# Making the skewed copies of the bias table: one transfer out of SBUF, or eight from DRAM to DRAM

## The chip, the cores and the metric

The kernel runs on 1 core of one Trainium2 chip. The metric is the device time of one execution in microseconds (us); less is better. TensorE (PE) multiplies, VectorE (DVE), ScalarE (ACT) and GpSimd (POOL) do the elementwise work, and SyncE (SP) issues the DMA transfers of this kernel, which 16 DMA engines carry out.

## The reference

Two transformer blocks run one after the other over 512 tokens of width 1024, all in float32. The first block has two layers (band attention, short convolution, gated mixing, feed-forward). The second has four kinds of attention, two of which add a bias that depends on the distance between query and key and on the head, 8 heads in all:

```python
def _t5_bias(table, dist):
    return jnp.moveaxis(table[_t5_bucket(dist)], -1, -3).astype(jnp.float32)
...
s = jnp.einsum('bhqmd,bhkmd->bhmqk', qb, k) * scale
s = s + _t5_bias(table, dist)[:, None]
s = jnp.where(dist >= 0, s, NEG)
```

The bias of a head is one function of the distance. Written as a row of 640 numbers (float32, 2560 bytes), the bias of a block of 128 queries is that row, shifted by one place from query to query.

## The kernel before

**Weights.** Every weight matrix is cut into units of 128 x 1024 float32 (512 KB). `Stream` loads unit after unit in the order of use into 3 `raw` buffers (L255, on SP's queue), and splits each into a rounded part `wh` on ACT (L267) and a remainder `wl` on DVE (L268). A product of a 128-column block with the activations is 24 matmuls of 128x512 (`mm_kb`, L514 to L516: 8 slices of the inner dimension by three products); `mblock` does that for one unit. `next` splits two units ahead of the one in use, and a `raw` buffer is loaded anew as soon as L268 has read it.

**The stage around the change.** After the first layer's band attention (whose last products run at about 271 us) come `bias_tables` and then the z stage of that layer: 8 column blocks, in each of which `mblock` makes a product, DVE scales it into `z` (L635) and ACT and DVE split the convolution's output `y` into two parts (L506, L507). The sigmoid of the `z` blocks runs on ACT (L378). The second layer has the same z stage, without `bias_tables`.

**The bias table.** `bias_tables` (L846) makes the 8 rows of 640 numbers by a small matmul with a one-hot matrix (L860), and ACT copies them to the tile `row` (L861): 8 partitions with 2560 bytes each. One DMA (L863) then writes 128 copies of each row to the DRAM tile `bias_d` [8, 128, 640], reading each partition of `row` 128 times: 2.6 MB. Much later, in the second block, `load_bias` (L865) reads 4 heads at a time from `bias_d`, with a row step of 639 instead of 640, which shifts each copy by one place.

**What sets the order.** The program writes instructions in the order of the source; a scheduler in the framework then simulates the program and orders each engine's instructions by when they are ready there, with the source order as priority. Each engine, and SP with its DMA issues too, then works through its list in order. DRAM tiles are tracked like others: a DMA that reads one waits on a semaphore until the DMA that wrote it has landed.

Of the kernel before, what the change touches and what calls it, by code (L numbers as in the profile page):

```python
# [9 lines left out]
F32 = mybir.dt.float32  # L10
# [4 lines left out]
P = 128  # L15
# [264 lines left out]
class Kern:  # L280
# [250 lines left out]
    def layer(self, l, tail, pend):  # L531
        nc = self.nc
        h = Pair(self, "h", NB)
# [100 lines left out]
        for m in range(NB):  # L634
            nc.vector.tensor_mul(z[m], self.mblock(h), self.R)  # L635
            self.split(yp.hi[m], yp.lo[m], y[m])
        op_ = Pair(self, "op", NB)
        for m in range(NB):
            self.act(z[m], z[m], AF.Sigmoid)
# [206 lines left out]
    def bias_tables(self):  # L846
        nc = self.nc
        oh = self.blk("oh", [33, 768], F32)
        nc.sync.dma_start(oh, self.a["onehot"])
        tab = self.small("tab", [33, 8], bufs=1)  # L850
        nc.sync.dma_start(tab, self.a["tab"])
        ohr = self.blk("ohr", [33, 768], F32R)
        nc.vector.tensor_copy(ohr, oh)
        tabr = [self.small(n, [33, 8], F32R, bufs=1) for n in ("tabh", "tabl")]
        self.split(*tabr, tab)
        row = self.blk("row", [8, 640], F32)
        for c0, c1, c2 in ((0, 512, 512), (512, 768, 640)):
            ps = self.ps("tb")
            for i, t in enumerate(tabr):
                nc.tensor.matmul(ps[0:8, :c1 - c0], t, ohr[:, c0:c1], start=i == 0, stop=i == 1)  # L860
            nc.scalar.copy(row[:, c0:c2], ps[0:8, :c2 - c0])  # L861
        self.bias_d = self.dramp.tile([8, P, 640], F32, name="bias_d")
        nc.sync.dma_start(self.bias_d, row[:, None, :].to_broadcast([8, P, 640]))  # L863

    def load_bias(self, h0):  # L865
        F = FM(self, "F", 4, F32)
# [856 lines left out]
```

## Time and profile before

| | us |
|---|---|
| median of 3 runs | 2506.98 (2504.95 to 2508.45) |
| the profiled execution's own time | 2510.06 |
| its span, from first to last instruction | 2508.3 |
| PE busy | 2416.4 (96% of the span) |
| DVE, ACT, POOL busy | 1354.6, 991.1, 424.2 |

The times of rows are counted from the start of the span. A chain of waits is followed back from the last instruction of a stretch, at each step to what released it. "Landing" is the time from a DMA's issue until its data is there. In a table by stretches, PEclk is the clock granted to TensorE as a share of full speed and DMA the mean busy share of the 16 DMA engines.

### The profile page before, as it was taken

What the parts mean: (1) busy time and instruction counts of PE and PEld (TensorE: products, weight loads), DVE (VectorE), ACT (ScalarE), POOL (GpSimd) and SP (SyncE); (2) the same over time, 40 slices, a digit from 0 to 9 for tenths busy, and PEclk for the clock granted to TensorE, in tenths of its full rate; (3) what the DMA queues carried; (4) which work ended last, traced back from release to release, by engine and by line L of the source; (5) the groups of instructions that cost most, each with busy time, mean ns of one, the idle gap of its engine ahead of it and who ended that gap; (6) DMA issues with size and microseconds to landing.
All of it is one profiled execution on the core that took longest, in us unless ns stands there. A gap on an engine that the chain in (4) does not pass through costs nothing.

```text
span 2508.3 us, 32433 instructions
## 1 busy us (share of the span) xinstructions
PE 2416.4 (96%) x12648; PEld 2078.5 (83%) x12648; DVE 1354.6 (54%) x2349; ACT 991.1 (40%) x1785; POOL 424.2 (17%) x454
## 2 busy tenths in 40 slices
PE   8999779999999999999999999999898899999999
PEld 7888658898888897888888988888797888988888
DVE  7777343356643258776433666422667686645431
ACT  4555232343223234555323422222276575333320
POOL 3423000121110015231011111100031442000000
PEclk9999989999999999999999999999899999999999
DMA  4222442245523231123323554322321214233250
GB/s 143 93 68 72 87 125 84 85 152 210 185 92 126 93 130 59 64 68 100 118 76 101 174 188 168 101 93 93 111 88 40 79 35 135 85 101 101 93 173 29
DMA packets 84857, 264.33 MB, mean 105 GB/s; under 512 B 9023, under 2 KB 17855, under 8 KB 84704
## 3 DMA queue, kind: packets, MB, share of 16 engines
q1 hardware_dynamic: 84704, 262.27, 31.9%
q8 instruction: 99, 1.62, 0.3%
q14 instruction: 54, 0.44, 0.1%
HBM read 247.03 MB, written 15.20 MB: 105 GB/s over the span
## 4 chain that ended last, share of the span: by engine, by line
PE 90%; DVE 5%; another core or an unknown queue 2%; ACT 2%; POOL 1%; issue 1%; DMA 0%; SPq 0%; DVEq 0%; ACTq 0%; POOLq 0%
PE ps L514 24%; PE ps L516 24%; PE ps L515 24%; PE hd L515 2%; PE hd L516 2%; PE hd L514 2%; PE o L821 1%; PE pt L796 1%; PE tm L998 1%; PE tm L999 1%; PE tm L1000 1%; PE s L772 1%; PE s L771 1%; PE s L1117 1%
## 5 line engine op out<-in xcount | busy, mean ns | idle before, releaser
L268 DVE TENSOR_TENSOR wl<-raw,wh 128x1024 fp32r<-128x1024 f32 x382 | 471.2, 1250 | 385.1 <-ACT wh L267 323.3
L267 ACT CAST wh<-raw 128x1024 fp32r<-128x1024 f32 x382 | 389.9, 1049 | 225.3 <-DMA raw<-in_w_dram 144.3
L514 PE MATMUL ps<-hh,wh 128*128 128x512 f32 x752 | 297.3, 396 | 34.2 <-ACT wh L267 34.2
L516 PE MATMUL ps<-hh,wl 128*128 128x512 f32 x752 | 298.0, 396 | 5.0 <-DVE wl L268 5.0
L515 PE MATMUL ps<-hl,wh 128*128 128x512 f32 x752 | 296.8, 395 | 0.0
L515 PE MATMUL ps<-hfl,wh 128*128 128x512 f32 x640 | 249.4, 390 | 0.0
L514 PE MATMUL ps<-hfh,wh 128*128 128x512 f32 x640 | 249.2, 390 | 0.0
L516 PE MATMUL ps<-hfh,wl 128*128 128x512 f32 x640 | 249.0, 389 | 0.0
L514 PEld LDWEIGHTS ps<-hh,wh 128*128 128x128 f32 x752 | 142.8, 190 | 62.2 <-ACT wh L267 35.1
L516 PEld LDWEIGHTS ps<-hh,wl 128*128 128x128 f32 x752 | 142.6, 190 | 34.5 <-DVE wl L268 7.3
L515 PEld LDWEIGHTS ps<-hl,wh 128*128 128x128 f32 x752 | 142.7, 190 | 27.9
L516 PE MATMUL ps<-hidh,wl 128*128 128x512 f32 (+1 forms) x396 | 145.1, 366 | 0.0
L514 PE MATMUL ps<-hidh,wh 128*128 128x512 f32 (+1 forms) x396 | 144.9, 366 | 0.0
L515 PE MATMUL ps<-hidl,wh 128*128 128x512 f32 (+1 forms) x396 | 144.7, 365 | 0.0
L516 PEld LDWEIGHTS ps<-hfh,wl 128*128 128x128 f32 x640 | 120.2, 188 | 25.0
L378 ACT ACTIVATE pp<-pp,at_nm 128x256 f32<-128x256 f32 (+1 forms) x208 | 114.4, 553 | 66.4 <-DVE at_nm L778 54.3
L515 PEld LDWEIGHTS ps<-hfl,wh 128*128 128x128 f32 x640 | 120.2, 188 | 24.6
L514 PEld LDWEIGHTS ps<-hfh,wh 128*128 128x128 f32 x640 | 120.0, 188 | 24.7
L701 POOL TENSOR_TENSOR gs<-gs,R 128x512 f32<-128x512 f32 x44 | 70.0, 1590 | 379.3 <-ACT gs L378 368.3
L515 PE MATMUL ps<-h3l,wh 128*128 128x512 f32 x320 | 124.5, 389 | 0.0
L516 PE MATMUL ps<-h3h,wl 128*128 128x512 f32 x320 | 124.5, 389 | 0.0
L514 PE MATMUL ps<-h3h,wh 128*128 128x512 f32 x320 | 124.3, 389 | 0.0
(439 smaller groups left out, 5251.9 us busy)
## 6 DMA issues: line engine op xcount, KB each, us to landing
raw<-in_w_dram SPq DMA_DIRECT2D x382, 512.0 KB, 3.7
adaraw<-in_ada_dram SPq DMA_DIRECT2D x48, 512.0 KB, 5.7
xd<-xh SPq DMA_DIRECT2D x24, 256.0 KB, 2.1
xh<-xd SPq DMA_DIRECT2D x24, 256.0 KB, 3.1
xh<-in_x_dram SPq DMA_DIRECT2D x16, 256.0 KB, 4.7
bias_d<-row SPq DMA_DIRECT2D x1, 2560.0 KB
xd<-fg SPq DMA_DIRECT2D x8, 256.0 KB, 3.2
F<-bias_d SPq DMA_DIRECT2D x8, 256.0 KB, 4.3
```

Of the source, the lines that this page charges most:

```text
L267: nc.scalar.copy(hi, raw)
L268: nc.vector.tensor_sub(lo, raw, hi.bitcast(F32))
L378: i = nc.scalar.activation(out, in_, func, **kw)
L514: nc.tensor.matmul(ps[:, t], w[0][:, sl], h.hi[kb][:, t], start=first, stop=False)
L515: nc.tensor.matmul(ps[:, t], w[0][:, sl], h.lo[kb][:, t], start=False, stop=False)
L516: nc.tensor.matmul(ps[:, t], w[1][:, sl], h.hi[kb][:, t], start=False, stop=last)
L701: nc.gpsimd.tensor_mul(g, g, self.R)
L771: nc.tensor.matmul(ps[:, :n], q, KH[g][:, LO[i]:HI[i]], start=True, stop=False)
L772: nc.tensor.matmul(ps[:, :n], q, KL[g][:, LO[i]:HI[i]], start=False, stop=True)
L796: nc.tensor.transpose(bank[:, c0:c0 + P], pslice(h, i)[:, c:c + P], self.ident)
L821: nc.tensor.matmul(ps[:, c0:c1], V[j][:, g * P:(g + 1) * P], t[b][:, a, c0:c1], start=(a == 0 and j == 0), stop=(a == 1 and j == 2))
L998: nc.tensor.matmul(o, h.hi[kb][:, tsl], w[0][:, sl], start=kb == 0 and i == 0, stop=False)
```

## The change

`bias_tables` now writes `row` once to a DRAM tile `row_d` [8, 640] (20 KB). The 128 copies of head h are made by `bias_copy(h)`, a DMA that reads row h of `row_d` 128 times and writes 128 rows of `bias_d` (320 KB). It is called once in each of the 8 column blocks of the first layer's z stage, behind the split of `y`.

```diff
         for m in range(NB):
             nc.vector.tensor_mul(z[m], self.mblock(h), self.R)
             self.split(yp.hi[m], yp.lo[m], y[m])
+            if l == 0:
+                self.bias_copy(m)
...
             nc.scalar.copy(row[:, c0:c2], ps[0:8, :c2 - c0])
+        self.row_d = self.dramp.tile([8, 640], F32, name="row_d")
+        nc.sync.dma_start(self.row_d, row)
         self.bias_d = self.dramp.tile([8, P, 640], F32, name="bias_d")
-        nc.sync.dma_start(self.bias_d, row[:, None, :].to_broadcast([8, P, 640]))
+
+    def bias_copy(self, h):
+        self.nc.sync.dma_start(self.bias_d[h], self.row_d[h:h + 1].to_broadcast([P, 640]))
```

## Rows read from the trace of the kernel before

**Rows 1.** The page: span, and busy time by engine.

```profile
span 2508.3 us, 32433 instructions
PE 2416.4 (96%) x12648; PEld 2078.5 (83%) x12648; DVE 1354.6 (54%) x2349; ACT 991.1 (40%) x1785; POOL 424.2 (17%) x454
```

**Rows 2.** Chain of waits, 250 to 420 us: start, length, what.

```profile
286.30 44.11 another core or an unknown queue
330.43 1.05 ACT wh L267
```

**Rows 3.** Waits, 255 to 360 us: who waited for whom, total, times, longest.

```profile
ACT wh L267 <- DMA raw<-in_w_dram: 47.8, 3, 44.1
...
PE ps L514 <- ACT wh L267: 31.3, 1, 31.3
```

**Rows 4.** PE in order of time: start, length, line, operation, idle before.

```profile
299.80 0.39 PE L516 MATMUL ps<-hh,wl 128*128 128x512 f32 x1
331.53 0.80 PE L514 MATMUL ps<-hh,wh 128*128 128x512 f32 x1 [31.34 <-ACT wh L267]
...
338.19 0.39 PE L514 MATMUL ps<-hh,wh 128*128 128x512 f32 x1
```

**Rows 5.** Stretches: PE, PEld, DVE, ACT, POOL busy; PEclk, DMA, GB/s last.

```profile
300.00:310.00 10.00, 0.19 (x1) 0.00 (x0) 0.00 (x0) 0.00 (x0) 0.00 (x0) 0.68 0.62 102
310.00:320.00 10.00, 0.00 (x0) 0.00 (x0) 0.00 (x0) 0.00 (x0) 0.00 (x0) 0.50 0.46 50
...
340.00:350.00 10.00, 10.00 (x45) 8.26 (x44) 4.96 (x8) 5.98 (x9) 0.00 (x0) 1.00 0.31 103
350.00:360.00 10.00, 10.00 (x46) 8.28 (x45) 8.57 (x11) 5.85 (x9) 0.00 (x0) 1.00 0.78 240
```

**Rows 6.** SP's DMA issues in order of time: start, length of the issue.

```profile
265.91 0.35 SPq L255 DMA_DIRECT2D raw<-in_w_dram  x1
274.36 0.83 SPq L863 DMA_DIRECT2D bias_d<-row  x1
275.46 19.33 SPq L255 DMA_DIRECT2D raw<-in_w_dram  x1
```

**Rows 7.** The tile raw, 275 to 277 us: landing of the load issued there.

```profile
DMA to landing us min/median/max: 54.9/54.9/54.9
```

**Rows 8.** DVE in order of time, first layer's z stage, then the second layer's.

```profile
278.47 0.69 DVE L635 TENSOR_TENSOR z<-ps,R 128x512 f32<-128x512 f32 x1 [3.04 <-PE ps L516]
280.28 2.35 DVE L268 TENSOR_TENSOR wl<-raw,wh 128x1024 fp32r<-128x1024 f32 x2
289.35 0.69 DVE L635 TENSOR_TENSOR z<-ps,R 128x512 f32<-128x512 f32 x1 [4.75 <-PE ps L516]
...
351.34 0.69 DVE L635 TENSOR_TENSOR z<-ps,R 128x512 f32<-128x512 f32 x1
...
1178.41 0.69 DVE L635 TENSOR_TENSOR z<-ps,R 128x512 f32<-128x512 f32 x1 [4.13 <-PE ps L516]
...
1216.49 0.69 DVE L635 TENSOR_TENSOR z<-ps,R 128x512 f32<-128x512 f32 x1
```

**Rows 9.** DMA issues of the page: engine, times, KB each, median us to landing.

```profile
raw<-in_w_dram SPq DMA_DIRECT2D x382, 512.0 KB, 3.7
...
xd<-xh SPq DMA_DIRECT2D x24, 256.0 KB, 2.1
...
bias_d<-row SPq DMA_DIRECT2D x1, 2560.0 KB
...
F<-bias_d SPq DMA_DIRECT2D x8, 256.0 KB, 4.3
...
out_dram<-xm SPq DMA_DIRECT2D x2, 128.0 KB, 1.7
```

**Rows 10.** The tile tab: its load from DRAM.

```profile
L851 SPq DMA_DIRECT2D tab<-in_tab_dram x1: 367/367/367, 7.5 to 7.5; - x1
```

**Rows 11.** ACT in order of time.

```profile
331.38 0.63 ACT L378 ACTIVATE z<-z 128x512 f32<-128x512 f32 x1
```

## The prediction

> **What bounds the kernel now.** I read the page first. PE is busy for 2416.4 of 2508.3 us [rows 1], so only some 92 us of the span can be won by taking waits away, and a change in a transfer is worth what it takes from those 92 us. The list of waits around the bias table shows that a third of them lies here: PE waited once for 31.3 us for the cast of a weight unit (`wh`), and that cast on ACT waited 44.1 us for its `raw` load [rows 3]. The chain of waits says the same: 44.11 us up to 330.43 us that no engine explains, then the cast [rows 2]. SP's list gives the cause. The bias transfer is issued at 274.36, the next weight load at 275.46; that load's issue alone takes 19.33 us [rows 6] and its data is there 54.9 us after issue [rows 7], where the median of the 382 weight loads is 3.7 us [rows 9]. In the stretch in which no engine works (310 to 320 us) the DMA engines are busy for 0.46 of their time and move 50 GB/s [rows 5]: about 7.4 of 16 engines, which fits a transfer of 8 partitions laid on 8 engines, each reading one partition over and over. At 50 GB/s its 2560 KB (2.62 MB) take 52 us, from about 275 to 328. A weight load has its share on those engines too, and stands behind it there.
>
> **What the stall costs.** PE's last matmul before it starts at 299.80, and matmuls follow each other every 0.2267 us at full speed: one block of 24 takes 5.44 us, as the second layer's z stage shows: (1216.49 - 1178.41) / 7 [rows 8]. The next would have started at 300.03. It starts at 331.53, and the first 15 run slowly: the granted clock was 0.50 in the idle stretch and is 1.00 from 340 us on (the levels of 1.2 and 2.4 GHz) [rows 5]. The sixteenth starts at 338.19 [rows 4]; without the stall it would at 300.03 + 15 x 0.2267 = 303.43. The loss is 34.8 us. A second way gives the same: from the first `z` to the eighth the first layer takes 351.34 - 278.47 = 72.87 us, the second, with the same stream of weight loads and no bias transfer, 38.08; the difference is 34.79 [rows 8]. Behind 340 us PE is the bound again, so what is won here arrives at the end.
>
> **The change, part by part.**
>
> *Removed*: the transfer L863, and with it the 34.8 us, if the eight new transfers don't bring part of them back.
>
> *Added: `row_d`*, 20 KB from 8 partitions. It is issued where L863 was, at 274.36, since ACT's copies into `row` are where they were. Nearest rows are stores to DRAM of 128 KB (1.7 us to landing) and 256 KB (2.1 us) [rows 9]; I take 2.
>
> *Added: a wait on SP*. The first copy may only be issued when `row_d` has landed, at about 276.4. SP works in order, so the weight loads listed behind that copy wait up to 2 us as well. PE doesn't see it: after L863 it worked for 25.8 us (274.4 to 300.2) on units loaded before. Seven more DMAs at 0.35 to 0.83 us of issue each [rows 6] are some 3 to 6 us of an SP that has little else to do.
>
> *Moved: the place of the copies*. The source has one in each column block, but a copy waits for nothing except `row_d`, and the scheduler issues what is ready: the load of `tab`, written in `bias_tables`, is issued at 7.5 us [rows 10]. So I expect not a spacing of 5.44 us but most of the eight close together from 276.4 on. The sum must hold in that case too.
>
> *Added: eight copies of 320 KB* (327,680 bytes) from DRAM to DRAM. No row of this trace has such a transfer. From below: the engines moved 240 GB/s at a share of 0.78 [rows 5], so 308 GB/s if all were busy, and a copy holds them for 1.1 us. From above: the share and rate of L863, 50 GB/s at 0.46, scaled to 16 busy engines are 109 GB/s, 3.0 us a copy; and if a copy is spread no better than L863, 50 GB/s, 6.6 us a copy, the same 52 us in all. Which of the two ceilings holds hangs on the spread. A transfer's outermost dimension was 8 in L863 and gave 7.4 busy engines; it is 128 in a copy, as in the weight loads and in the load of `F`, whose 256 KB land after 4.3 us [rows 9], latency included. I take 1.5 us a copy, nearest to the rows of loads and stores with 128 rows, 12 us in all, and keep 1.1 and 6.6 as ends.
>
> The Trainium skill has a rule for the spread: "DMA: Bandwidth & Descriptors", section "Why a DMA increments its semaphore by 16 and not by 1", says that a transfer uses the largest number of engines up to 16 that divides the slowest dimension of both sides, so 8 for L863 and 16 for a copy. The share of 0.46 agrees with its 8; that a step of zero on the source side counts as a dimension of 128 no run here shows yet. By the rule the 6.6 us fall away.
>
> *How much the copies may take before PE notices.* The load issued at 275.46 must land at 298.9 (300.03 less the 1.10 us from the cast's start to PE's, 330.43 to 331.53 [rows 2, 4]). It is ready for issue while SP waits for `row_d` or before. The second load's buffer is free at about 281.5, when the first of the two subtractions of L268 ends [rows 8]; it is needed one block later, at 304.4. If all copies are in front of it, 276.4 + 8C + 3.7 must be below 304.4: C up to 3.0 us a copy costs nothing. My 1.5 is half of that. If the copies are spread over the blocks, C may be larger still.
>
> *What is late next*: nothing in the z stage. The second layer's runs at PE's pace with the same loads [rows 8]. The order of the lists behind the stage should stay nearly as it is: ACT's list has the cast of the late unit ahead of the sigmoid of the third `z`, which was ready at 290.04 (289.35 + 0.69 [rows 8]) and ran at 331.38 [rows 11], so the order was laid down by a simulation that didn't see the stall.
>
> **Sum.** 2510.06 (the profiled execution) - 34.8 = 2475.3. The median of the runs shown is 3.08 below that execution, so the forecast for a median is 2472.2 us.
>
> **The rivals.**
>
> *A: the copies are slow, and part of the stall stays.* For it: one row read 128 times is what L863 did, at 50 GB/s; nothing here has read the same DRAM bytes again and again. Against it: the spread over 128 rows. At 4 us a copy in one burst the stall is 8 x 4 - 24.3 = 7.7 us and the slow restart 3.4, so 2483; at 5 us 2491. Spaced by blocks, even 6.6 us a copy costs less: 6.6 + 2.1 for a weight load (at 240 GB/s [rows 5]) against 5.44 a block is 3.3 us in each of 8, 26 in all, of which some 20 of reserve are taken off: 6 us and the restart, 2482. In a burst 6.6 us a copy leaves 28.5 + 3.4 of 34.8, 2504: no change.
>
> *B: all 128 reads of a copy fall on one place in DRAM, and it serves them one after the other.* L863 had eight rows read side by side, 6 GB/s each; a copy has all engines on one row of 2560 bytes. Slower than before from 8C - 24.3 + 3.4 = 34.8 on, 7.0 us a copy. At 10 us it is 2531; if a row is served at the 6 GB/s of a partition in L863, 52 us a copy, some 2870. Against it: the 128 rows of `F` and the weight units come at full speed; but they are different bytes, so no row excludes it. The Trainium skill, "DMA: Bandwidth & Descriptors", section "Latency and other measured facts", has DRAM copies falling from 207 to 103 GB/s per direction when their rows' step makes them meet in the same part of the memory, and calls the mechanism an inference. No run here shows it; by its 103 GB/s a copy would take an estimated 3.2 us and the result would be about 1 to 5 us above my forecast.
>
> *C: the spacing isn't what the source says.* The burst that I expect; it changes nothing below 3.0 us a copy.
>
> **How the numbers follow.** From the spread of the runs shown (2504.95 to 2508.45), 0.2% or 5 us is about what can be told from no change. No stall left: 0.70, its own range 2466 to 2479 (half a per cent for a changed order of lists and the spread of the runs). Rival A: 0.18, from 2476 to 2504, of which 0.04 within 0.2% of before. Rival B: 0.09. A reordering behind the stage that costs all of the gain: 0.03, about 0.02 of it within 0.2% of before and 0.01 slower. Faster by over 0.2%: 0.70 + 0.14 = 0.84; within: 0.04 + 0.02 = 0.06; slower: 0.09 + 0.01 = 0.10. The range of 2464 to 2493 takes in the first case and A up to 5 us a copy.
>
> **What would show it right or wrong.** Right: from the first `z` to the eighth of the first layer 38 us; PE's wait of 31.3 us for the cast gone; eight rows of 320 KB with landings of a few us, close together; weight loads between 275 and 320 us landing within some 20 us. Wrong: landings of a copy that grow by over 3 us from one to the next, a DMA share far below 1 while copies are in flight, the granted clock again at 0.50 near 310 us, or a new wait of PE behind 340 us.

## The result, and the profile after

The kernel takes 2472.78 us after the change (median of 4 runs, 2471.46 to 2476.64) against 2505.97 before: a ratio of 0.9866, with a 95% interval of 0.9851 to 0.9882. The forecast was 2472.2. The profiled execution took 2472.93 us.

The page, which answers to [rows 1]: PE's busy time is nearly the same, the span is 37.1 us shorter, and 60.9 us of it are left in which PE isn't busy.

```profile
span 2471.2 us, 32444 instructions
PE 2410.3 (98%) x12648; PEld 2075.6 (84%) x12648; DVE 1354.4 (55%) x2349; ACT 991.2 (40%) x1785; POOL 425.3 (17%) x454
```

The chain of waits from 250 to 420 us, by line, where [rows 2] had 44 us that no engine explained. It is now matmuls from end to end:

```profile
by line: PE ps L514 32.2%; PE ps L515 32.1%; PE ps L516 32.1%; PE o L823 2.1%; PE pt L798 1.3%; PE tb L862 0.5%
```

The first and the last `z` of the first layer on DVE, which answer to [rows 8]: 317.06 - 278.98 = 38.08 us, the second layer's time to the hundredth, and 34.79 less than before.

```profile
278.98 0.69 DVE L635 TENSOR_TENSOR z<-ps,R 128x512 f32<-128x512 f32 x1 [3.03 <-PE ps L516]
...
317.06 0.69 DVE L635 TENSOR_TENSOR z<-ps,R 128x512 f32<-128x512 f32 x1
```

SP's list, which answers to [rows 6]. One weight load is issued while SP waits for `row_d` (it is the one that stood behind L863 and took 54.9 us; it lands after 3.2 us now); then all eight copies (L869) in 5.27 us, in one burst and not one per column block; then weight loads as their buffers come free.

```profile
274.87 0.30 SPq L865 DMA_DIRECT2D row_d<-row  x1
275.98 0.33 SPq L255 DMA_DIRECT2D raw<-in_w_dram  x1
276.44 5.27 SPq L869 DMA_DIRECT2D bias_d<-row_d  x8
282.25 12.14 SPq L255 DMA_DIRECT2D raw<-in_w_dram  x4
```

The stretches of the burst, with the columns of [rows 5]. The 16 DMA engines are full (shares of 0.98 and 1.01) and move 300 to 308 GB/s, where L863 kept 0.46 of them busy for 50 GB/s; PE runs through at full clock.

```profile
280.00:285.00 5.00, 5.00 (x24) 4.14 (x23) 3.72 (x5) 1.28 (x2) 0.00 (x0) 1.00 0.98 308
285.00:290.00 5.00, 5.00 (x24) 4.15 (x23) 0.25 (x2) 2.61 (x4) 0.00 (x0) 1.00 1.01 300
290.00:295.00 5.00, 5.00 (x24) 4.15 (x23) 4.03 (x5) 1.68 (x2) 0.00 (x0) 1.00 0.43 143
```

The landing of the weight load issued at 282.25. It is the first that stands behind the whole burst, as the load of [rows 7] with its 54.9 us stood behind L863:

```profile
DMA to landing us min/median/max: 9.4/9.4/9.4
```

So it is there at 291.65, about 12 us before PE would miss it. The copies themselves land 5.7 to 9.3 us after their issue.

**The 2.3 us beyond the stage.** The spans fell by 37.1 us and the stage by 34.8, but the medians only by 33.2: the profiled execution of the kernel before took 2510.06 us, more than any of its four other runs (2503.93 to 2508.45). Some 1.5 us of the rest lie in one gap of PE at the start of the feed-forward part. These are the stretches there: the kernel before, the kernel after, and two kernels of the experiments below, spaced (no stall) and heads_from_sbuf (a longer stall than before):

```profile
530.00:535.00 5.00, 4.01 (x24) 3.81 (x23) 5.00 (x13) 5.00 (x11) 0.89 (x1) 0.74 0.86 301
```

```profile
495.70:500.70 5.00, 4.02 (x32) 3.76 (x31) 5.00 (x13) 5.00 (x11) 0.89 (x1) 1.00 0.89 302
```

```profile
496.30:501.30 5.00, 4.01 (x22) 3.81 (x21) 5.00 (x13) 5.00 (x11) 0.89 (x1) 0.66 0.88 305
```

```profile
565.30:570.30 5.00, 4.01 (x32) 3.75 (x31) 5.00 (x13) 5.00 (x11) 0.89 (x1) 1.00 0.87 303
```

PE is busy for the same 4 us each time, but with 22 or 24 matmuls where the mean granted clock is 0.66 or 0.74, and with 32 where it is 1.00. The lower clock is there in spaced, which has no stall, and not in heads_from_sbuf, which has one. So it doesn't go with the stall, and nothing here counts these 1.5 us as won by the change. The cause of the fall is open.

### The profile page after: what moved, and what is told of

Same layout as the page of the kernel before. It is cut to its first block, busy times and chain, and to the rows that moved or that the text cites. A ratio compares the mean times of both kernels' runs of the same rounds, so it can differ in the third digit from the quotient of the medians.

```text
span 2471.2 us, 32444 instructions
## 1 busy us (share of the span) xinstructions
PE 2410.3 (98%) x12648; PEld 2075.6 (84%) x12648; DVE 1354.4 (55%) x2349; ACT 991.2 (40%) x1785; POOL 425.3 (17%) x454
## 4 chain that ended last, share of the span: by engine, by line
PE 92%; DVE 5%; ACT 1%; POOL 1%; issue 1%; DMA 0%; SPq 0%; DVEq 0%; POOLq 0%; ACTq 0%
PE ps L514 24%; PE ps L516 24%; PE ps L515 24%; PE hd L515 2%; PE hd L516 2%; PE hd L514 2%; PE o L823 2%; PE pt L798 1%; PE tm L1004 1%; PE tm L1005 1%; PE tm L1006 1%; PE s L774 1%; PE s L773 1%; PE s L1123 1%; PE pc L407 1%
## 5 line engine op out<-in xcount | busy, mean ns | idle before, releaser
L514 PE MATMUL ps<-hidh,wh 128*128 128x512 f32 (+1 forms) x396 | 145.1, 366 | 0.0
```

What stands on the lines that cost most here:

```text
L514: nc.tensor.matmul(ps[:, t], w[0][:, sl], h.hi[kb][:, t], start=first, stop=False)
```

## The experiments

All were run beside the kernel before, whose medians in the three groups were 2507.82, 2508.57 and 2507.67 us. The theory: L863 was slow because of its source, few SBUF partitions read over and over, and weight loads stood behind it in one queue. The rivals: its spread over 8 engines; the cost of the eight new transfers themselves; the spacing. The edits of dram_heads_outer, rows_step2, rows_step4, act_queue and one_dma are made to the kernel before, the others to the kernel after.

**heads_from_sbuf: eight transfers, but out of SBUF**

```diff
-        self.row_d = self.dramp.tile([8, 640], F32, name="row_d")
-        nc.sync.dma_start(self.row_d, row)
+        self.row = row
...
-        self.nc.sync.dma_start(self.bias_d[h], self.row_d[h:h + 1].to_broadcast([P, 640]))
+        self.nc.sync.dma_start(self.bias_d[h:h + 1], self.row[h:h + 1, None, :].to_broadcast([1, P, 640]))
```

> Eight transfers as after the change, but each reads its head's partition of the SBUF tile row, without row_d. Theory 1 (the source was the limit: one SBUF partition read over and over gives about 6 GB/s, 50 GB/s over 8): a copy of 327,680 bytes takes 13 us if the limit belongs to a group of partitions, 52 us if to the partition; 105 to 420 us in all, a long stall again, 2540 to 2860 us and slower than before. Rival (the spread was the limit: 8 engines instead of 16): 3.0 us a copy, 24 us in all, 2472 to 2477 us, as after the change.

Measured: 2544.02 us, ratio 1.0145 (1.013 to 1.016), slower than before. A stretch of it, and PE's wait:

```profile
285.00:290.00 5.00, 5.00 (x23) 4.14 (x23) 1.56 (x3) 0.38 (x1) 0.00 (x0) 1.00 0.91 27
```

```profile
PE ps L514 <- ACT wh L267: 64.9, 2, 61.5
```

A share of 0.91 is 14.6 of 16 engines, so the wide spread is there, and still they get 27 GB/s out of one partition. The spread isn't the limit; the source is. At 27 GB/s a copy takes 12 us, 97 us in all: the price named for a group of partitions.

**dram_heads_outer: the spread of before, out of DRAM**

```diff
-        nc.sync.dma_start(self.bias_d, row[:, None, :].to_broadcast([8, P, 640]))
+        self.row_d = self.dramp.tile([8, 640], F32, name="row_d")
+        nc.sync.dma_start(self.row_d, row)
+        nc.sync.dma_start(self.bias_d, self.row_d[:, None, :].to_broadcast([8, P, 640]))
```

> One transfer as before the change, heads outermost, but out of the DRAM tile row_d. Theory 1 (source): even on 8 engines the copies run at some 150 to 200 GB/s, 13 to 17 us in all, inside the reserve of 24 us, 2472 to 2475 us. Rival (spread): half the engines at the old rate, 50 us, the wait of PE of some 30 us stays, 2503 to 2507 us. The DMA share while it runs tells whether 8 engines (about 0.5) or 16 (about 1.0) work.

Measured: 2473.1 us, ratio 0.9862 (0.9845 to 0.9878), the whole gain, with no wait of PE in the stage. A stretch of it between two weight loads:

```profile
280.00:282.00 2.00, 2.00 (x10) 1.65 (x10) 2.00 (x3) 0.96 (x2) 0.00 (x0) 1.00 0.51 195
```

A share of 0.51 is near the 0.46 of L863, but at 195 GB/s instead of 50. Eight engines suffice once the source is DRAM.

**rows_step2 and rows_step4: out of SBUF, with the rows further apart**

The transfer and queue of before; only the 8 rows lie on every second or every fourth partition (for step 4):

```diff
-        tabr = [self.small(n, [33, 8], F32R, bufs=1) for n in ("tabh", "tabl")]
-        self.split(*tabr, tab)
-        row = self.blk("row", [8, 640], F32)
+        tabr = [self.small(n, [33, 32], F32R, bufs=1) for n in ("tabh", "tabl")]
+        for t in tabr:
+            nc.vector.memset(t.bitcast(F32), 0.0)
+        self.split(*[t[:, 0:32:4] for t in tabr], tab)
+        row = self.blk("row", [32, 640], F32)
...
-        nc.sync.dma_start(self.bias_d, row[:, None, :].to_broadcast([8, P, 640]))
+        nc.sync.dma_start(self.bias_d, row[0:32:4, None, :].to_broadcast([8, P, 640]))
```

> The kernel before with its one transfer out of SBUF, but the 8 rows lie on partitions 0, 2, ... 14 (the small matmul makes 16 rows, of which every second is used). Theory (a group of 4 neighbouring partitions gives about 27 GB/s: one partition read by 16 engines gave 27 to 28, eight neighbours gave 50): 4 groups, about 100 GB/s, 26 us in all, done at about 301 where the first weight load behind it is needed at 298.9: a stall of 4 to 8 us with a slow restart, 2479 to 2486 us. Rival (8 engines reading SBUF in that shape give 50 GB/s wherever the rows lie): no change, 2505 to 2509 us.

> The same with the rows on partitions 0, 4, ... 28: 8 groups. Theory: the groups no longer limit, 8 engines run at 150 to 200 GB/s, 13 to 17 us in all, no stall, 2471 to 2476 us, as after the change and without a DRAM row table. Rival: no change, 2505 to 2509 us.

Measured: step 2 2481.89 us (0.989, 0.9875 to 0.9905), step 4 2472.97 us (0.9853, 0.9838 to 0.9868). Stretches early in the transfer, before the first weight load moves, step 2 and then step 4, and PE's wait with step 2 (with step 4 there is none in the stage):

```profile
277.00:287.00 10.00, 10.00 (x45) 8.27 (x45) 4.86 (x6) 3.26 (x6) 0.00 (x0) 1.00 0.47 100
```

```profile
276.00:281.00 5.00, 5.00 (x24) 4.14 (x23) 2.53 (x4) 1.88 (x3) 0.00 (x0) 1.00 0.52 207
```

```profile
PE ps L514 <- ACT wh L267: 4.9, 1, 4.9
```

At a share of 0.46 to 0.52 throughout, the rate is 50 GB/s with neighbouring rows [rows 5], 100 with step 2 and 207 with step 4: some 25 GB/s for each group of four partitions that holds a row (2, 4 and 8 groups). With step 4 the groups need not be the limit any more, since 8 engines moved 195 GB/s out of DRAM too. That a group is four partitions the runs alone don't show: groups of eight at 50 GB/s, with 27 for a single partition, would fit them as well. The change's gain can be had without any DRAM row table, and without a changed order: here the weight load still stands behind the transfer in SP's queue, as before, and lands after 16.5 us.

**act_queue: the slow transfer on another queue**

```diff
-        nc.sync.dma_start(self.bias_d, row[:, None, :].to_broadcast([8, P, 640]))
+        nc.scalar.dma_start(self.bias_d, row[:, None, :].to_broadcast([8, P, 640]))
```

> The transfer of before, unchanged in source and shape, but issued from ACT's queue instead of SP's. If the stall was weight loads standing in order behind the transfer in one queue: loads and transfer share the engines by turns, loads land after 5 to 10 us, no stall or one of a few us, 2472 to 2480 us. Rival (the engines themselves are held by the slow reads, whichever queue they come from): loads land after 40 us or more, 2500 to 2507 us.

Measured: 2493.21 us, ratio 0.994 (0.9925 to 0.9955): between the two, in neither range. PE's wait, and the landing of the four weight loads issued from 275 to 300 us:

```profile
PE ps L514 <- ACT wh L267: 15.4, 1, 15.4
```

```profile
DMA to landing us min/median/max: 17.5/19.3/20.4
```

Out of SP's queue the loads land after 17 to 20 us instead of 54.9: longer than their usual 3.7, but nearly soon enough. The last of the four was issued at 297.5 and landed 19.0 us later, at 316.5, just as PE ran out of work; with 1.1 us for the cast, late loads alone would have cost about 1 us (an estimate from these times). The cast of that unit ran 14.5 us after its load had landed, and what it waited for was the bias transfer itself:

```profile
330.96 1.04 ACT L267 CAST wh<-raw 128x1024 fp32r<-128x1024 f32 x1 [25.68 <-DMA bias_d<-row]
```

`row` and `wh` come from one pool of SBUF buffers (`blk`), and in this program the `wh` of that cast is the next tile in the buffer of `row`. It can't be written before the slow transfer has read `row` for the last time. So the transfer stalls PE in two ways: by the loads behind it in SP's queue, and by the buffer that it holds. In the kernel before the second is hidden behind the first. After the change `row` is free as soon as the 20 KB of `row_d` have landed.

**one_copy, spaced and one_dma: does the burst of eight cost anything?**

```diff
 one_copy:
-            if l == 0:
+            if l == 0 and m == 0:
...
-            a = self.bias_d[h0 + h]
+            a = self.bias_d[0]
 spaced:
-            self.k.nc.sync.dma_start(t, self.w[u])
+            self.last = self.k.nc.sync.dma_start(t, self.w[u])
...
-        self.nc.sync.dma_start(self.bias_d[h], self.row_d[h:h + 1].to_broadcast([P, 640]))
+        i = self.nc.sync.dma_start(self.bias_d[h], self.row_d[h:h + 1].to_broadcast([P, 640]))
+        self.order(i, self.st.last)
 one_dma:
-        nc.sync.dma_start(self.bias_d, row[:, None, :].to_broadcast([8, P, 640]))
+        self.row_d = self.dramp.tile([8, 640], F32, name="row_d")
+        nc.sync.dma_start(self.row_d, row)
+        nc.sync.dma_start(self.bias_d.rearrange("h p c -> p h c"), self.row_d[None, :, :].to_broadcast([P, 8, 640]))
```

> After the change, but only head 0's copies are made, and all heads read them (the output differs). If the eight transfers cost nothing: 2471 to 2475 us, the same as after the change, with 320 KB moved instead of 2.6 MB. Rival (they still hide a cost of some us, in late weight loads or in the clock): 2 to 6 us below it.

> After the change, with each head's transfer put behind a weight load in SP's list, so that one load stands between any two (the spacing that the source shows). If the burst costs nothing: 2471 to 2476 us, the same as after the change, with the loads of the stage landing sooner than 9 us. Rival (burst delays something unseen): 1 to 4 us below it.

> One transfer out of row_d for all heads, the 128 copies outermost and the heads inside. If source and spread are all that counts: 9 to 12 us of all 16 engines, 2471 to 2476 us, the same as after the change with one issue instead of eight. Rival (the split into eight transfers is part of the gain, since loads get between them): a wait of PE of some us, 2477 us or more.

Measured: one_copy 2473.22 us (0.9861, 0.9846 to 0.9876), spaced 2471.56 (0.9851, 0.9835 to 0.9868), one_dma 2472.43 (0.9857, 0.9842 to 0.9872). None can be told from the change. In spaced the copies do stand between loads, and the loads from 274 to 320 us land sooner (6.1 us at most, against 9.8 after the change):

```profile
DMA to landing us min/median/max: 3.2/4.5/6.1
```

In all three PE has no wait in the stage. So the eight transfers are hidden, as far as such runs can tell (about 4 us), and neither their number nor their place is part of the gain.

**copies_x3 and copies_x12: how much the stage can hide**

```diff
         self.nc.sync.dma_start(self.bias_d[h], self.row_d[h:h + 1].to_broadcast([P, 640]))
+        for i in range(2):
+            x = self.dramp.tile([P, 640], F32, name=self.n("bias_x"))
+            self.nc.sync.dma_start(x, self.row_d[h:h + 1].to_broadcast([P, 640]))
```

(and `range(11)` for twelve)

> After the change, with each head's transfer made three times (two of them to DRAM tiles that nothing reads): 24 transfers, 7.9 MB. At 308 GB/s, the rate of the burst after the change, they take 26 us; ten or eleven stand before the second and third weight load, the rest between later ones, so each load is still in time: 2471 to 2476 us, no change from one set. Rival (reserve of 24 us is the limit for all of them at once, whatever stands between): a stall of 2 to 6 us with a slow restart, 2476 to 2483 us.

> After the change, with each head's transfer made twelve times: 96 transfers, 31 MB, 102 us of all engines at 308 GB/s, beside 8 weight loads of 1.7 us. PE has 43.5 us of work in the stage and some 24 us of reserve: a stall of 42 to 52 us comes back, 2515 to 2530 us, slower than before. Rival (DRAM serves one row's reads slowly when they pile up): far more, over 2560 us.

Measured: threefold 2477.7 us (0.9878, 0.9864 to 0.9893), twelvefold 2624.98 us (1.0467, 1.0451 to 1.0483). PE's wait for casts with three and with twelve sets, and 20 us of the twelvefold kernel:

```profile
PE ps L514 <- ACT wh L267: 2.2, 1, 2.2
```

```profile
PE ps L514 <- ACT wh L267: 124.4, 8, 18.6
```

```profile
280.00:300.00 20.00, 20.00 (x89) 16.54 (x89) 6.78 (x9) 4.44 (x7) 0.00 (x0) 1.00 1.00 146
```

The threefold kernel came out in its rival's range: 24 copies, 26 us at 308 GB/s, just pass the reserve, though nine of them stood ahead of the second weight load and the rest between later ones. The twelvefold kernel came out far above what I expected, at a full DMA share and half the rate. Its transfers read one row twelve times in succession, and that was the rival B of the prediction; the next two kernels ask for it.

**row0_only and x12_rotated: reading one row of DRAM**

```diff
 row0_only:
-        self.nc.sync.dma_start(self.bias_d[h], self.row_d[h:h + 1].to_broadcast([P, 640]))
+        self.nc.sync.dma_start(self.bias_d[h], self.row_d[0:1].to_broadcast([P, 640]))
 x12_rotated (against copies_x12):
-            self.nc.sync.dma_start(x, self.row_d[h:h + 1].to_broadcast([P, 640]))
+            self.nc.sync.dma_start(x, self.row_d[(h + i + 1) % 8:(h + i + 1) % 8 + 1].to_broadcast([P, 640]))
```

> After the change, but all eight transfers read row 0 of row_d (the output differs). Theory (reads of one 2560-byte row in DRAM have a ceiling of about 140 GB/s, which twelve transfers of one row in succession showed, and which eight rows side by side did not): about 140 to 180 GB/s at a full DMA share, some 16 to 19 us in all, still inside the reserve, 2471 to 2476 us. Rival (the twelvefold kernel was slow for its many destinations): 300 GB/s as after the change, 9 us in all, the same time.

> The twelvefold kernel with the same 96 transfers, but successive ones read successive rows of row_d. Theory (ceiling of one row): near 300 GB/s again, a stall of 42 to 55 us, 2515 to 2535 us. Rival (destinations, or the pile of transfers itself): as the twelvefold kernel, 2615 to 2630 us.

Measured: row0_only 2471.34 us (0.9851, 0.9835 to 0.9868), x12_rotated 2541.24 us (1.0124, 1.0109 to 1.014). Two stretches of row0_only's burst:

```profile
280.00:285.00 5.00, 5.00 (x24) 4.14 (x23) 1.28 (x2) 2.41 (x4) 0.00 (x0) 1.00 1.02 141
285.00:290.00 5.00, 5.00 (x24) 4.14 (x23) 2.69 (x4) 0.84 (x2) 0.00 (x0) 1.00 1.00 150
```

And x12_rotated, the same 20 us as above and PE's wait:

```profile
280.00:300.00 20.00, 20.00 (x90) 16.57 (x89) 7.70 (x11) 6.58 (x10) 0.00 (x0) 1.00 0.97 300
```

```profile
PE ps L514 <- ACT wh L267: 45.4, 6, 8.0
```

The same 96 transfers move 300 GB/s when successive ones read different rows, 146 when they read the same one; eight copies of one row instead of eight rows fall from 308 to 141. So one row of DRAM does have a ceiling, about 141 to 150 GB/s, or 2.2 to 2.3 us a copy. The wait of 45.4 us is inside the 42 to 55 that I gave for x12_rotated; its time is a little above. In the profiled executions, from the first `z` to the last block of the next eight (L642), it takes 145.1 us where the kernel after takes 81.6. Of these 63.5 us 45.4 are the waits; the other 18 are matmuls at the lower clock, about 3 us after each of six waits, which I had counted once.

## Why the prediction was right, point by point

**The stall and its price: right.** 34.8 us were predicted for the stage and 34.79 measured. The sum for the profiled execution was 2475.3 and it took 2472.93; some 1.5 us of the rest are the clock at one gap behind the stage. That the median came out within 0.6 us of the forecast is in part luck: runs of one kernel lie about 5 us apart, and the medians fell by 33.2 us, not 34.8. That L863 also held a buffer that PE's work needed (act_queue) isn't in the prediction; it cost nothing there, since that wait lay inside the same 34.8 us.

**`row_d` and SP's wait: right.** The first copy was issued at 276.44, predicted 276.4; a weight load went out while SP waited. The near agreement is luck: `row_d` went out 0.5 us later than assumed, and 1.6 us, not 2, passed until the first copy.

**The burst (rival C): right.** The eight came within 5.27 us; spaced shows that their place makes no difference.

**The size of a copy: too large, at no cost.** I took 1.5 us; 327,680 bytes at 308 GB/s are 1.06, the lower end that I had kept.

**The reserve: right in size.** 24.3 us were worked out for copies in front of the second load. Eight copies cost nothing, 24 of them (26 us) cost a wait of 2.2 us. Since not all 24 stood ahead of the second load, that bears out the size and no more.

**Why the copy is faster than L863: wrong in its reason.** The forecast was right without it, since every rate from 109 GB/s up was inside the reserve. The prediction let the choice between its two upper ends hang on the spread, 8 engines or 16. dram_heads_outer keeps the spread of L863 and has the whole gain, heads_from_sbuf has the wide spread and is slower than before. The limit was the source: L863's rows lay in two groups of four SBUF partitions, at about 25 GB/s each (50 in all; 27 from one). The Trainium skill, "DMA: Bandwidth & Descriptors", section "Why a DMA increments its semaphore by 16 and not by 1", counted the engines rightly (0.46 and 0.51 with 8 outermost, 0.98 to 1.01 with 128, also where the source steps by zero), but the number of engines didn't decide. What decided stands on another of its pages, "SBUF — State Buffer", section "Door 1: The DMA port swizzle": four neighbouring partitions share a port for DMA. The traces agree: one partition 27 GB/s, eight neighbours 50, every second 100, every fourth 207. By these rates the 50 GB/s of L863 belonged to its source and said nothing of a source in DRAM: the end of 6.6 us had no ground, and rival A little.

**Rival A: fell.** No part of the stall stayed.

**Rival B: there, but small.** One row read by all engines is served at 141 to 150 GB/s, 2.2 to 2.3 us a copy; the point from which it would have decided was 7.0. In the change itself, successive copies read different rows and the ceiling doesn't show.

## What to carry to other kernels

A transfer that nobody waits for can still stop the kernel, if loads that somebody needs stand behind it in the same queue: look at the landing times of the loads next to it, not at its own. It also keeps the buffer that it reads, and whoever gets that buffer next waits for it (act_queue). Ask first where its bytes come from: a broadcast out of a few neighbouring SBUF partitions ran at some 25 GB/s for each group of four that held a row, with 8 engines or with 16; spread the rows by four partitions or go by DRAM. And work out how many microseconds of transfer the prefetched units cover; inside that reserve, order and number of the transfers are free.

## What the runs showed of the hardware that was not expected

- 16 DMA engines read one SBUF partition over and over at 27 GB/s and a share of 0.91; a high share says little of the rate.
- DRAM to DRAM copies of 2560-byte rows run at 300 to 308 GB/s, but at 141 to 150 when all read one row.
- With the slow transfer in another queue, weight loads beside it landed after 17 to 20 us instead of 54.9. What was left of PE's wait (15.4 of 31.3 us) was, all but about 1 us, for the buffer that the transfer read.
